# Layer B's in-projections of blocks 1 to 3 as seven half-size products, with weight operands kept in DRAM

## The chip, the cores and the metric

The kernel runs on one core of a Trainium2 chip. The metric is the device time of one execution in microseconds; the time before is the median of three runs. The profile is of one further execution.

## What is computed

One inference step of two layers over 2048 prompt tokens and 64 sample tokens (8 sequences of 8), model width 1024. Layer A (gated DeltaNet) is not changed. Layer B is a retention layer, whose four in-projections take the normed input to queries, keys, values and gates:

```python
p = _rmsnorm(x, norm_w) @ w_in.astype(F32)                 # 1024 -> 2*1024 + 2*2048
q, k, v, gate = jnp.split(p, [B_QK, 2 * B_QK, 2 * B_QK + B_VW], axis=-1)
q = _rotary(q, pos0);  k = _rotary(k, pos0) * (B_DK ** -0.5)   # 4 heads of 256
o, S = _retention_chunked(q, k, v, S0)                     # v: 4 heads of 512, S: 256 x 512
o = _rmsnorm(o, onorm_w) * jax.nn.silu(gate)
y = x + (o.reshape(B, L, B_VW) @ w_out.astype(F32))
```

A final norm follows. The retention states of the prompt and of all sample sequences are outputs too.

## The kernel before

All matrix work is in float32 split into two float32r parts, hi and lo: a product is three matmuls (hi·hi, hi·lo, lo·hi, the table `PASSES`), which accumulate in PSUM. `wload` (L177) loads one raw weight tile of 128 x 1024 into a ring of two buffers named wraw, casts it on ScalarE (hi, L181) and subtracts on VectorE (lo, L182) into a ring of w tiles. `split` (L194, recorded as L195 and L196) does the same for activations.

The prompt is cut into four blocks of 512 tokens (n = 0 to 3). In layer B each block goes through four heads (h = 0 to 3). For a head the program writes, in this order: four gate tiles and two tiles each of Q and K with `colproj` (L236), 24 matmuls of 512 columns each (8 tiles of the inner width by 3 passes); rotation (`rope`, L975); a wait for the last head's retention; V in four PSUM banks, 96 matmuls; then `flush_B` (L1224), the out-projection `outproj_B` (L1153) of the head before, 8 output tiles of 12 matmuls, which adds into the residual xa in SBUF; then the head's own retention `ret_prompt` (L1002) is put on a list of tasks. At h = 3 `build_xn` (L264) makes the next block's normed operands before the out-projection. One head of each block is sampled: its projections are 576 columns wide, as two halves of 288, and `ret_sample` (L1059) follows, which loads and stores 16 state tiles.

The order of the work comes from two places. A list of tasks, `_Pipe` (L36), holds generators with a priority; `pump` runs those whose time has come on a clock that each written matmul moves on, and `wait` runs tasks until one is done. Under it the tile framework schedules the instructions and gives each engine one fixed order. On the chip each engine, and SP's queue of transfers, keeps that order. A buffer of a ring is given out again when everything that read it is done. `pp` (L117) has three PSUM banks, which in-projections and out-projection share; `xst` (L167) is a ring of three 128 x 576 buffers in layer B.

```python
    def wload(src):
        raw = sb.tile([128, 1024], F32, tag="wraw", bufs=2, name="wraw")
        w = wtile()
        nc.sync.dma_start(raw, src)
        ACT.copy(w[:, 0, :], raw)
        V.tensor_tensor(w[:, 1, :], raw, w[:, 0, :].bitcast(F32), op=ALU.subtract)
        return w
```

Of the kernel before, what the change touches and what calls it, by code (L numbers as in the profile page):

```python
# [16 lines left out]
D = 1024  # L17
# [70 lines left out]
def tile_hybrid(ctx: ExitStack, tc: tile.TileContext, a: dict, S: int):  # L88
# [49 lines left out]
    x1_d = dr.tile([D, S + NS], F32, name="x1_d")  # L138

# [25 lines left out]
    wn, xn_ = [0, 2], [0, 3]  # L165
# [700 lines left out]
    wn[1], xn_[1] = 3, 4  # L866
# [83 lines left out]
    def finish_A():  # L950
        wn[:], xn_[:] = [0, 2], [0, 3]
# [9 lines left out]
    def open_B():  # L961
        finish_A()
        pb = ctx.enter_context(tc.tile_pool(name="pb", bufs=1))
        B.pb = pb
        B.rmask = const("rmask", (128, 4, 128), a["rmask"], pb)
# [9 lines left out]
    def rope(pair, c, sn, outs, lo, hi, v=lambda t: t):  # L975
        for (p0, s, e), (p1, _, _) in zip(pieces(pair[0], lo, hi), pieces(pair[1], lo, hi)):
            n = e - s
            for out, (f0, f1), op in ((outs[0], (c, sn), ALU.subtract), (outs[1], (sn, c), ALU.add)):
                t = [sb.tile([128, XC], F32, tag="tmp", bufs=2, name="rt")[:, :n] for _ in range(2)]
                V.tensor_tensor(t[0], p0, f0[:, s:e], op=ALU.mult)  # L980
                V.tensor_tensor(t[1], p1, f1[:, s:e], op=ALU.mult)  # L981
                V.tensor_tensor(out(s, e), v(t[0]), v(t[1]), op=op)
# [19 lines left out]
    def ret_prompt(n, h, QR, KR, Vt, GT, OG):  # L1002
        pb, S_ = B.pb, B.S[h]
        gC = float(gam[h] ** 128)
        for c in range(4):
# [28 lines left out]
            for i, (al, vl) in enumerate(PASSES):  # L1034
                mm(o, Ah[:, al], Vt[:, c, vl], start=(first and i == 0), stop=(i == 2))
            yield from until(posts[-1])
            on = ret_on(o, h, 0)
            for k in range(2):
                p = po("p") if k == 0 else pf("p")
                for i, (al, vl) in enumerate(PASSES):  # L1040
                    mm(p, Kt[:, al, k * 128 : (k + 1) * 128], Vt[:, c, vl], start=(i == 0), stop=(i == 2))
# [17 lines left out]
    def ret_sample(h, QRs, KRs, vraw, GTs, OG, rms):  # L1059
        pb = B.pb  # L1060
        g8 = float(gam[h] ** 8)
# [91 lines left out]
    def outproj_B(h, OG, xa, width, acc):  # L1153
        sacc = B.pb.tile([128, 256], F32, tag="rms", name="sacc")[:, :NS] if h == 0 and width > TB else None
        for cp in range(4):
            w = wload(a["w_out_b"][h, cp])
            for ci in range(2):
# [3 lines left out]
                for p, s, e in pieces(pst, 0, TB):  # L1161
                    V.tensor_tensor(xa[:, ct, s:e], xa[:, ct, s:e], p, op=ALU.add)  # L1162
                if acc is not None:
                    sqsum(acc[:, :TB], xa[:, ct, :], ct)
                if width > TB:
                    (p, _, _), = pieces(pst, TB, XC)
                    V.tensor_tensor(B.xas[:, ct, :], B.xas[:, ct, :], p, op=ALU.add)  # L1167
                    if sacc is not None:
# [308 lines left out]
```

## Time and profile before

| | |
|---|---|
| median of three runs | 3317.8 us (3315.15 to 3319.45) |
| profiled execution | 3320.3 us, span 3318.5 us |
| TensorE busy | 3231.2 us, 97% |
| VectorE, ScalarE, POOL busy | 66%, 44%, 7% |
| DMA | 379.8 MB, 114 GB/s |

The span is the time from the first to the last instruction; the execution's own time is 1.8 us more. Shares of busy time are averages over stages: layer A fills the first part up to some 1430 us, layer B the rest, where a head of a block takes a little over 100 us. The views used below are the page itself, the chain of waits (what work or wait each moment of the end time hangs on), groups of instructions by shape with their mean time, transfers with their time from issue to landing, and tables of busy time by stretch.

### The profile page before, as it was taken

To read this page: it belongs to the slowest core of one execution; us is meant where nothing else is said; L and a number is where in the kernel's file an instruction comes from. 1 tells how busy PE (TensorE), PEld (TensorE's weight loads), DVE (VectorE), ACT (ScalarE), POOL (GpSimd) and SP (SyncE) were. 2 spreads that over 40 slices of the span, in tenths; PEclk is the share of its full clock that TensorE was granted. 3 is DMA by queue.
4 is the path that set the end of the run, shared out by engine and by line. 5 is a ranking of instruction groups with operands and counts; after the bars stand their busy time and mean duration, and the time that the engine had idled before them with its cause. 6 is when DMAs were issued, how large, how long until landed. Compare 5 with 4: busy or idle time off the path is not lost.

```text
span 3318.5 us, 50681 instructions
## 1 busy us (share of the span) xinstructions
PE 3231.2 (97%) x18847; PEld 2700.4 (81%) x18847; DVE 2198.3 (66%) x4943; ACT 1453.5 (44%) x3243; POOL 240.2 (7%) x501
## 2 busy tenths in 40 slices
PE   7999999999999999999999999999999999999998
PEld 7999787778788888788888788877888788878886
DVE  6876778688878877755555665556564656575556
ACT  7655555465545645333333442343342433343333
POOL 1221011001110000000000000000000000000000
PEclk9999999999999999999999999999999999999999
DMA  4333454435444343552223442126232523253222
GB/s 134 96 101 85 144 167 142 132 106 152 130 129 126 89 143 99 151 162 82 74 82 106 129 163 89 59 83 194 77 116 82 171 68 116 71 175 117 89 77 70
DMA packets 241111, 379.78 MB, mean 114 GB/s; under 512 B 100688, under 2 KB 130144, under 8 KB 240864
## 3 DMA queue, kind: packets, MB, share of 16 engines
q1 hardware_dynamic: 240864, 376.54, 37.6%
q8 instruction: 148, 2.42, 0.3%
q14 instruction: 99, 0.81, 0.1%
HBM read 318.90 MB, written 55.46 MB: 113 GB/s over the span
## 4 chain that ended last, share of the span: by engine, by line
PE 83%; DVE 6%; DMA 4%; ACT 3%; POOL 1%; issue 1%; SPq 0%; DVEq 0%; POOLq 0%; ACTq 0%
PE pp L97 53%; PE pv L97 10%; PE o L97 5%; PE p L97 5%; PE kyd L97 2%; PE oT L106 1%; DMA st<-in_state_ret 1%; PE kp L97 1%; DVE w L182 1%; PE ap L97 1%; POOL so L572 1%; PE kq L97 1%; PE os L97 1%; ACT on L569 1%; PE pvs L97 1%
## 5 line engine op out<-in xcount | busy, mean ns | idle before, releaser
L97 PE MATMUL pp<-xn,w 128*128 128x512 f32 (+1 forms) x7760 | 1648.5, 362 | 13.2 <-ACT w L181 4.2
L97 PEld LDWEIGHTS pp<-xn,w 128*128 128x128 f32 x7760 | 1267.3, 189 | 210.2 <-issue 13.9
L181 ACT CAST w<-wraw 128x1024 fp32r<-128x1024 f32 x416 | 436.8, 1050 | 691.4 <-PE pp L97 449.0
L182 DVE TENSOR_TENSOR w<-wraw,w 128x1024 fp32r<-128x1024 f32 x416 | 508.4, 1222 | 249.1 <-ACT w L181 248.0
L97 PE MATMUL pp<-OG,w 128*128 128x512 f32 (+1 forms) x2880 | 582.6, 360 | 6.3 <-DVE xas L1167 3.2
L97 PEld LDWEIGHTS pp<-OG,w 128*128 128x128 f32 x2880 | 482.0, 190 | 89.8 <-issue 3.6
L97 PE MATMUL pv<-w,xn 128*128 128x512 f32 x1536 | 370.8, 396 | 0.0
L97 PEld LDWEIGHTS pv<-w,xn 128*128 128x128 f32 x1536 | 287.1, 188 | 73.8 <-issue 5.0
L1162 DVE TENSOR_TENSOR xa<-xa,pp 128x512 f32<-128x512 f32 (+2 forms) x160 | 90.2, 579 | 137.2 <-PE pp L97 137.1
L728 DVE SCALAR_TENSOR_TENSOR acc<-pp,cw,acc 128x511 f32<-128x511 f32 (+2 forms) x216 | 160.4, 742 | 22.0 <-ACT acc L725 21.7
L990 POOL TENSOR_TENSOR so<-oss,rsc 128x1 f32<-128x1 f32 x72 | 17.8, 247 | 1412.5 <-ACT on L988 1412.5
L981 DVE TENSOR_TENSOR rt<-pp,cs 128x512 f32<-128x512 f32 (+2 forms) x80 | 46.3, 578 | 105.9 <-PE pp L97 105.9
L473 DVE TENSOR_TENSOR VP<-VP,tm 128x66 f32<-128x66 f32 (+26 forms) x510 | 106.5, 209 | 4.4
L471 DVE TENSOR_TENSOR tm<-LP,VP 128x66 f32<-128x66 f32 (+26 forms) x510 | 104.3, 204 | 4.4
L97 PE MATMUL p<-Vt,Kt 128*128 128x512 f32 x384 | 104.4, 405 | 0.6 <-ACT on L992 0.6
L195 ACT CAST OG<-og 128x256 fp32r<-128x256 f32 x192 | 71.7, 405 | 62.0 <-DVE og L628 33.4
L97 PE MATMUL o<-Sc,Qc 128*128 128x512 f32 x360 | 93.4, 394 | 0.0
L196 DVE TENSOR_TENSOR OG<-og,OG 128x256 fp32r<-128x256 f32 x192 | 75.4, 420 | 20.8 <-ACT OG L195 20.5
L106 PE MATMUL oT<-ident,on 128*128 128x128 f32 x432 | 73.1, 276 | 11.4 <-DVE on L573 9.5
L97 PEld LDWEIGHTS p<-Vt,Kt 128*128 128x128 f32 x384 | 68.2, 189 | 13.0 <-ACT on L992 0.9
L106 PEld LDWEIGHTS oT<-ident,on 128*128 128x128 f32 x432 | 52.6, 140 | 31.9 <-DVE on L573 14.6
L97 PEld LDWEIGHTS o<-Sc,Qc 128*128 128x128 f32 x360 | 66.6, 188 | 14.4
(369 smaller groups left out, 3947.3 us busy)
## 6 DMA issues: line engine op xcount, KB each, us to landing
wraw<-in_w_in_a SPq DMA_DIRECT2D x128, 512.0 KB, 3.7
wraw<-in_w_qkg SPq DMA_DIRECT2D x128, 512.0 KB, 3.6
wraw<-in_w_v SPq DMA_DIRECT2D x64, 512.0 KB, 3.7
wraw<-in_w_out_b SPq DMA_DIRECT2D x64, 512.0 KB, 3.6
wraw<-in_w_out_a SPq DMA_DIRECT2D x32, 512.0 KB, 3.7
st<-in_state_ret SPq DMA_DIRECT2D x64, 256.0 KB, 3.6
out_ret_s<-st SPq DMA_DIRECT2D x64, 256.0 KB, 2.7
LP<-sl SPq DMA_DIRECT2D x72, 128.0 KB, 2.9
```

The source lines that it names most:

```text
L97: ins = nc.tensor.matmul(out, lhsT, rhs, start=start, stop=stop)
L106: ins = nc.tensor.transpose(out, x, ident[:p, :p])
L181: ACT.copy(w[:, 0, :], raw)
L182: V.tensor_tensor(w[:, 1, :], raw, w[:, 0, :].bitcast(F32), op=ALU.subtract)
L195: ACT.copy(hi, x)
L196: V.tensor_tensor(lo, x, hi.bitcast(F32), op=ALU.subtract)
L471: V.tensor_tensor(tv, LP[:, m, m + 1 : m + 1 + n].unsqueeze(2).to_broadcast([128, n, ncol]), VP[:, m, 0:ncol].unsqueeze(1).to_broadcast([1 ...
L473: V.tensor_tensor(VP[:, m + 1 : m + 1 + n, 0:ncol], VP[:, m + 1 : m + 1 + n, 0:ncol], tv, op=ALU.subtract)
L569: ACT.activation(on[:, j, :], o[:, j, :], AF.Square, scale=128.0 ** -0.5, accum_out=ss[:, j : j + 1])
L728: V.scalar_tensor_tensor(acc[:, sh:], ap[:, : TB - sh], cw[:, ct, j : j + 1], acc[:, sh:], op0=ALU.mult, op1=ALU.add)
L981: V.tensor_tensor(t[1], p1, f1[:, s:e], op=ALU.mult)
L1162: V.tensor_tensor(xa[:, ct, s:e], xa[:, ct, s:e], p, op=ALU.add)
```

## The change

For blocks 1 to 3 each in-projection of a head is cut in two by two by two: output rows, inner width and tokens in halves. Seven products of half size with sums of weight quarters and of input quarters take the place of eight. The matmuls have 256 columns: 12 in a product of gates, Q or K (`quad`, four per head with seven products each), 24 in one of V (`vquad`, seven products). `seven` adds the products up on VectorE, POOL and ScalarE in temporaries that use the wraw ring: in V the first buffer holds P1, P5 and then U3, the second U2 and U4.

The weight operands (A11, four sums, A12, A22, each as hi and lo) are made once by `prep`, 24 preparations with a task of the lowest priority (9) that starts with `open_B` in block 0. Each loads two weight tiles, forms four sums on POOL, splits seven operands and writes seven slots of 512 KB to DRAM. In blocks 1 to 3 `wstream` loads 42 slots per head into a ring of three w tiles. `build_halves` makes the input operands; three of its tiles have the buffers that `prep` uses (ta, tb, tc), so it waits for the last preparation.

To make room in SBUF, the residual goes through DRAM (x2_d) and the ring xst, the retention state is stored and loaded per head (sr_d), the samples of all four heads are worked in block 0, and V is split per chunk in `ret_prompt`. The task clock counts 0.455 ns a column in the place of 0.4167.

```diff
-        pipe.t += (max(0.4167 * n, 107.0) if rhs.dtype == F32R else max(1.667 * n, 110.0)) / 1000.0
+        pipe.t += (max(0.455 * n, 107.0) if rhs.dtype == F32R else max(1.667 * n, 110.0)) / 1000.0
...
+    x2_d = dr.tile([D, S + NS], F32, name="x2_d")
+    sr_d = dr.tile([BH, 128, 1024], F32, name="sr_d")
+    wh_d = [dr.tile([56, 128, 1024], F32, name=f"wh_d{h}") for h in range(BH)]
...
     def finish_A():
-        wn[:], xn_[:] = [0, 2], [0, 3]
+        wn[:], xn_[:] = [0, 2], [0, 2]
...
     def open_B():
...
+        B.pb = wp[0] = pb
+        wn[1] = 3
...
-        S23 = pb.tile([128, 2, 2, 512], F32, name="S23")
-        B.S = [pb.tile([128, 2, 512], F32, name=f"Sr{h}") for h in range(2)] + [S23[:, 0], S23[:, 1]]
-        B.xas = pb.tile([128, 8, NS], F32, name="xas")
-        nc.sync.dma_start(B.xas, x1_d[:, S : S + NS].rearrange("(k p) t -> p k t", p=128))
...
+    def prep(h, slots, src, vkind):
+        pb = B.pb
+        R = pb.tile([128, 2, 1024], F32, tag="ta", name="Rw")
+        for j in range(2):
+            nc.sync.dma_start(R[:, j, :], src[j])
...
+        yield 4.0
+        PL.tensor_tensor(sm[0], A21, A22, op=ALU.add)
+        PL.tensor_tensor(sm[1], sm[0], A11, op=ALU.subtract)
+        PL.tensor_tensor(sm[2], A11, A21, op=ALU.subtract)
+        PL.tensor_tensor(sm[3], A12, sm[1], op=ALU.subtract)
+        ops = [A11, sm[0], sm[1], A12, sm[2], sm[3], A22]
+        for i, x in enumerate(ops):
+            if i % 2 == 0:
+                o2 = pb.tile([128, 2, 2, 512], F32R, tag="tc", name="Wo")
+            o = o2[:, i % 2]
+            hi, lo = (v3(o[:, j, :], 256) if vkind else o[:, j, :] for j in range(2))
+            split(hi, lo, x)
+            nc.sync.dma_start(wh_d[h][slots[i]], o.rearrange("p t c -> p (t c)").bitcast(F32))
+            yield 1.5
...
+    def wstream(h):
+        for s in range(0, 56, 2):
+            w = wtile()
+            for j in range(2):
+                nc.sync.dma_start(w[:, j, :].bitcast(F32), wh_d[h][s + j])
+            for j in range(2):
+                yield v3(w[:, j, :], 512)
+    def build_halves(n, rb):
...
+        for kt in range(4):
+            xs, t = [], []
+            for k in (kt, kt + 4):
+                x = xst("xs")
+                nc.sync.dma_start(x[:, :TB], x1_d[k * 128 : (k + 1) * 128, n * TB : (n + 1) * TB])
+                y = sb.tile([128, XC], F32, tag="tmp", bufs=2, name="xt")
+                V.scalar_tensor_tensor(y[:, :TB], x[:, :TB], nw[:, 1, k : k + 1], rb[:, :TB],
+                                       op0=ALU.mult, op1=ALU.mult)
+                xs.append(x)
+                t.append(y)
+            lo_, hi_ = xn[kt], xn[kt + 4]
+            split(lo_[:, 0, l], lo_[:, 1, l], t[0][:, l])
+            split(hi_[:, 0, :TB], hi_[:, 1, :TB], t[1][:, :TB])
+            V.tensor_tensor(xs[0][:, l], t[0][:, r], t[0][:, l], op=ALU.subtract)
+            V.tensor_tensor(xs[0][:, r], t[1][:, r], xs[0][:, l], op=ALU.subtract)
+            V.tensor_tensor(xs[1][:, l], t[1][:, r], t[0][:, r], op=ALU.subtract)
+            V.tensor_tensor(xs[1][:, r], t[1][:, l], xs[0][:, r], op=ALU.subtract)
+            split(lo_[:, 0, r], lo_[:, 1, r], xs[0][:, l])
+            split(T2[:, kt, 0], T2[:, kt, 1], xs[0][:, r])
+            split(T3[:, kt, 0], T3[:, kt, 1], xs[1][:, l])
+            split(N4[:, kt, 0], N4[:, kt, 1], xs[1][:, r])
...
+    def seven(product, temp, put):
+        p1, p5, u2, u4 = (temp(j) for j in range(4))
+        ACT.copy(p1, product("b11"))
+        ACT.copy(p5, product("t1"))
+        V.tensor_tensor(u2, product("t2"), p1, op=ALU.add)
+        put(0, 0, product("b21"), p1, V)
+        PL.tensor_tensor(u4, u2, p5, op=ALU.add)
+        u3 = temp(0)
+        V.tensor_tensor(u3, product("t3"), u2, op=ALU.add)
+        put(1, 1, u3, p5, PL)
+        put(0, 1, product("b22"), u4, V)
+        put(1, 0, product("n4"), u3, V)
+    def quad(ws, xo, put):
+        def product(x):
+            w, bank = next(ws), pp("sq")[:, :256]
+            for kt in range(4):
+                for i, (wl, xl) in enumerate(PASSES):
+                    mm(bank, w[:, wl, kt * 128 : (kt + 1) * 128], xo[x](kt, xl),
+                       start=(kt == 0 and i == 0), stop=(kt == 3 and i == 2))
+                if kt % 2:
+                    pipe.pump()
+            return bank
+        temps = sb.tile([128, 1024], F32, tag="wraw", bufs=2, name="ptmp")
+        seven(product, lambda j: temps[:, 256 * j : 256 * j + 256], put)
+    def vquad(ws, xo, Vt):
+        def product(x):
+            w, bank = None, pp("sv")
...
+        temps = [sb.tile([128, 1024], F32, tag="wraw", bufs=2, name="ptmp") for _ in range(2)]
+        seven(product, lambda j: v3(temps[j // 2][:, 512 * (j % 2) : 512 * (j % 2) + 512], 256),
+              lambda i, j, x, y, eng: eng.tensor_tensor(Vt[:, 2 * j : 2 * j + 2, 256 * i : 256 * i + 256], x, y,
+                                                        op=ALU.add))
...
     def ret_prompt(n, h, QR, KR, Vt, GT, OG, S_):
...
+            Vh = pb.tile([128, 2, 512], F32R, tag="Vh", name="Vh")
+            split(Vh[:, 0], Vh[:, 1], Vt[:, c])
...
+        else:
+            nc.sync.dma_start(sr_d[h], S_.rearrange("p k v -> p (k v)"))
...
     def outproj_B(n, h, OG, width, acc):
+        src = x1_d if h == 0 else x2_d
...
+                xs = xst("xr")
+                nc.sync.dma_start(xs[:, :TB], src[rows, n * TB : (n + 1) * TB])
...
+                for p, s, e in pst:
+                    V.tensor_tensor(xs[:, s:e], xs[:, s:e], p[:, : e - s], op=ALU.add)
+                nc.sync.dma_start(x2_d[rows, n * TB : (n + 1) * TB], xs[:, :TB])
...
     def final(n, acc, samp):
...
+            xs = xst("xf")
+            nc.sync.dma_start(xs[:, :TB], x2_d[rows, n * TB : (n + 1) * TB])
...
     for n in range(NB):
         for h in range(4):
-            samp = (3 - h) * NB // 4 == n
+            samp = n == 0
...
+            if n:
+                S_ = pb.tile([128, 2, 512], F32, tag="Sr", bufs=2, name="Sr")
+                nc.sync.dma_start(S_.rearrange("p k v -> p (k v)"), sr_d[h])
+                ws = wstream(h)
...
+                    quad(ws, xo, put)
...
             if start:
                 open_B()
...
+                for j in range(BH):
+                    ptask = pipe.add(prep_head(j), 9, [ptask])
...
             if h == 3 and n + 1 < NB:
-                nxt = build_xn(x1_d, n + 1, 1, rb, XC)
+                pipe.wait(ptask)
+                xo = build_halves(n + 1, rb)
```

Three places of the engines' orders. First SP's queue around a V stage of a late head, before, where a row is a transfer with its target and source:

```order
L180 DMA wraw<-in_w_qkg 128x1024 x3
L1057 DMA out_ret_p<-Sr_16785 128x2x512
L180 DMA wraw<-in_w_qkg 128x1024
L180 DMA wraw<-in_w_v 128x1024 x4
L180 DMA wraw<-in_w_out_b 128x1024 x4
L180 DMA wraw<-in_w_qkg 128x1024 x7
```

and the same with the change, in block 1 (w are the ready operands, wh_d their place in DRAM):

```order
L1206 DMA sr_d<-Sr 128x1024
L1040 DMA w<-wh_d_75 128x1024 x23
L1409 DMA Sr<-sr_d 128x1024
L183 DMA wraw<-in_w_out_b 128x1024 x4
L1319 DMA x_d<-xr 128x512 x2
L1314 DMA xr<-x_d 128x512
```

The out-projection's raw weights stand behind V's weights in both; with the change their first buffer is a temporary of V, and residual tiles are loaded and stored between.

Second, TensorE from the end of a V stage into the out-projection, with the change (sv are V's products, o, p and kT belong to the retention, pp<-OG is the out-projection):

```order
L97 MATMUL sv<-w,tc 128x256 x12
L97 MATMUL ap<-QR,KR 128x128
L97 MATMUL sv<-w,tc 128x256 x12
L97 MATMUL o<-Vh,Ah 128x512
L97 MATMUL p<-Vh,Kt 128x512 x2
L106 MATMUL kT<-ident,KR 128x128
L97 MATMUL o<-Vh,Ah 128x512 x2
L97 MATMUL pp<-OG_23854,w 128x512 x4
L97 MATMUL p<-Vh,Kt 128x512
```

Before, the out-projection follows V's last matmul at once; now five matmuls and a transpose of the head's own retention stand between.

Third, the end of block 0 with the change, on SP (Rw and Wo are a preparation's raw weights and operands, xs the next block's input, xr the residual of the out-projection):

```order
L1003 DMA Rw<-in_w_v 128x1024 x2
L1024 DMA wh_d_76<-Wo 128x1024 x7
L1058 DMA xs<-x_d 128x512 x5
L1314 DMA xr<-x_d 128x512
L1316 DMA xr<-x_d 128x64
```

and on VectorE a little later:

```order
L199 TENSOR_TENSOR ta<-xs,ta 128x256
L199 TENSOR_TENSOR tb<-xs,tb 128x256
L199 TENSOR_TENSOR tc<-xs,tc 128x256
L1318 TENSOR_TENSOR xr<-xr,pp 128x288 x2
L1197 TENSOR_TENSOR og<-oT,GT 128x512 x2
L1318 TENSOR_TENSOR xr<-xr,pp 128x288 x2
```

The six preparations of head 3 stand on SP one behind the other, each two loads and seven writes, this one last; the block's input and the residual of the out-projection come after them, and so do their sums on VectorE.

## Rows read from the trace of the kernel before

**Rows 1.** The page: TensorE, and the span in 40 slices.
```profile
PE 3231.2 (97%) x18847; PEld 2700.4 (81%) x18847; DVE 2198.3 (66%) x4943; ACT 1453.5 (44%) x3243; POOL 240.2 (7%) x501
...
PE   7999999999999999999999999999999999999998
...
PEclk9999999999999999999999999999999999999999
```

**Rows 2.** Chain of waits, a head of block 3: start us, us, what.
```profile
3087.84 20.22 PE pp L97 x87
3108.06 22.32 PE pv L97 x96
3130.39 25.19 PE pp L97 x108
...
3156.24 4.18 PE pp L97 x18
3160.42 2.09 PE o L97 x9
...
3164.57 4.18 PE pp L97 x18
```

**Rows 3.** Busy us by engine, clock, DMA share, GB/s: the same head.
```profile
3088.00:3196.00 108.00, 108.00 (x487) 87.76 (x486) 58.51 (x90) 37.45 (x64) 2.94 (x8) 1.00 0.27 83
```

**Rows 4.** Chain of waits, in-projection of a sampled head, 288 columns.
```profile
1752.11 15.43 PE pp L97 x114
```

**Rows 5.** Groups by shape: xcount | busy us, mean ns | idle before, releaser.
```profile
L181 ACT CAST w<-wraw 128x1024 fp32r<-128x1024 f32 x416 | 436.8, 1050 | 691.4 <-PE pp L97 449.0 <-PE pv L97 121.2 <-PE pvs L97 62.4
...
L195 ACT CAST Sc<-Sr 128x512 fp32r<-128x512 f32 x60 | 35.0, 621 | 7.2 <-PE o L97 6.9
...
L182 DVE TENSOR_TENSOR w<-wraw,w 128x1024 fp32r<-128x1024 f32 x416 | 508.4, 1222 | 249.1 <-ACT w L181 248.0
L196 DVE TENSOR_TENSOR OG<-og,OG 128x256 fp32r<-128x256 f32 x192 | 75.4, 420 | 20.8 <-ACT OG L195 20.5
...
L196 DVE TENSOR_TENSOR Sc<-Sr,Sc 128x512 fp32r<-128x512 f32 x60 | 40.6, 686 | 6.9 <-ACT Sc L195 6.8
...
L1248 POOL MEMSET QRs<- 128x512 f32 x4 | 2.1, 530 | 111.0 <-PE os L97 66.6 <-PE pp L97 44.4
```

**Rows 6.** Transfers: xcount, KB each, median us from issue to landing.
```profile
wraw<-in_w_out_b SPq DMA_DIRECT2D x64, 512.0 KB, 3.6
...
x_d<-xr SPq DMA_DIRECT2D x32, 256.0 KB, 3.3
xs<-x_d SPq DMA_DIRECT2D x32, 256.0 KB, 3.6
...
out_ret_p<-Sr SPq DMA_DIRECT2D x2, 512.0 KB, 2.8
```

**Rows 7.** By stretch: a gap of TensorE and the clock after it.
```profile
2301.40:2304.70 3.30, 0.05 (x2) 0.05 (x1) 3.30 (x7) 1.34 (x2) 0.00 (x0) 1.00 0.43 143
2304.70:2306.00 1.30, 0.76 (x3) 0.53 (x4) 1.30 (x2) 0.00 (x0) 0.00 (x0) 0.88 0.14 50
2306.00:2309.00 3.00, 3.00 (x13) 3.00 (x14) 2.02 (x5) 0.30 (x1) 0.00 (x0) 0.50 0.80 194
2309.00:2312.00 3.00, 3.00 (x23) 2.88 (x23) 0.88 (x3) 0.00 (x0) 0.00 (x0) 0.98 0.39 156
```

**Rows 8.** By stretch: most bytes in 6 us, and in 22 us.
```profile
1482.00:1488.00 6.00, 6.00 (x27) 4.86 (x26) 1.23 (x1) 1.24 (x2) 0.00 (x0) 1.00 1.04 386
...
1479.80:1502.00 22.20, 22.20 (x99) 18.03 (x99) 7.83 (x9) 6.48 (x9) 0.00 (x0) 1.00 0.70 233
```

**Rows 9.** By stretch: a sampled head's in-projection, then the head after it.
```profile
1666.00:1781.00 115.00, 114.31 (x675) 101.95 (x674) 58.87 (x101) 37.29 (x71) 3.77 (x8) 1.00 0.25 75
1781.00:1910.00 129.00, 127.73 (x582) 98.40 (x581) 84.90 (x138) 51.63 (x95) 4.06 (x10) 1.00 0.43 136
```

**Rows 10.** Chain of waits, the end: last matmuls to last output.
```profile
3281.27 21.99 PE pp L97 x93
...
3309.91 0.75 DVE xa L1188
...
3311.32 3.95 DVE xa L1188 x6
```

More of the change, by code (lines that the diff above doesn't have):

```diff
@@ L976, in rope @@
         for (p0, s, e), (p1, _, _) in zip(pieces(pair[0], lo, hi), pieces(pair[1], lo, hi)):
[L977 to L982, printed above, removed]
+            rope_to(p0, p1, c[:, s:e], sn[:, s:e], [out(s, e) for out in outs], v)
@@ new lines, in rope_to, with rope_in @@
+    def rope_to(p0, p1, c, sn, outs, v=lambda t: t):
+        n = c.shape[1]
+        for out, (f0, f1), op in ((outs[0], (c, sn), ALU.subtract), (outs[1], (sn, c), ALU.add)):
+            t = [sb.tile([128, XC], F32, tag="tmp", bufs=2, name="rt")[:, :n] for _ in range(2)]
+            V.tensor_tensor(t[0], p0, f0, op=ALU.mult)
+            V.tensor_tensor(t[1], p1, f1, op=ALU.mult)
+            V.tensor_tensor(out, v(t[0]), v(t[1]), op=op)
+    def rope_in(x, c, sn):
+        t = [sb.tile([128, XC], F32, tag="tmp", bufs=2, name="rt")[:, :TB] for _ in range(2)]
+        V.tensor_tensor(t[0], x[:, 0], c, op=ALU.mult)
+        V.tensor_tensor(t[1], x[:, 1], sn, op=ALU.mult)
+        V.tensor_tensor(x[:, 0], x[:, 0], sn, op=ALU.mult)
+        V.tensor_tensor(x[:, 1], x[:, 1], c, op=ALU.mult)
+        V.tensor_tensor(x[:, 1], x[:, 1], x[:, 0], op=ALU.add)
+        V.tensor_tensor(x[:, 0], t[0], t[1], op=ALU.subtract)
@@ L1034, in ret_prompt @@
             for i, (al, vl) in enumerate(PASSES):
-                mm(o, Ah[:, al], Vt[:, c, vl], start=(first and i == 0), stop=(i == 2))
+                mm(o, Ah[:, al], Vh[:, vl], start=(first and i == 0), stop=(i == 2))
             yield from until(posts[-1])
@@ L1151, in ret_sample, with outproj_B @@
             post(ret_post(on, fin))
-    def outproj_B(h, OG, xa, width, acc):
-        sacc = B.pb.tile([128, 256], F32, tag="rms", name="sacc")[:, :NS] if h == 0 and width > TB else None
+    def outproj_B(n, h, OG, width, acc):
+        src = x1_d if h == 0 else x2_d
         for cp in range(4):
@@ L1182, in final @@
         yield 3.0
[L1183 to L1185 removed]
+        rb = bcast_rstd(rr, rr[:64, 4:5] if samp else None, "rbF")
         for k in range(8):
             rows = slice(k * 128, (k + 1) * 128)
[L1188 to L1189 removed]
@@ L1252, in tile_hybrid @@
-            for d in range(4):
-                if h == 0 and d == 0:
-                    ahead = colproj2([wload(a["w_qkg"][16 + 4 * h + j]) for j in range(2)], xk, width)
-                pst = ahead.pop(0) if ahead else colproj(a["w_qkg"][16 + 4 * h + d], xk, width)
-                for p, s, e in pieces(pst, 0, TB):
-                    ACT.activation(GT[:, d, s:e], p, AF.Silu)
-                V.tensor_scalar(GT[:, d, :], GT[:, d, :], onB[:, h, d : d + 1], None, op0=ALU.mult)
-                if samp:
+            if start:
+                xn_[:] = [0, 2]
+                stash = sb.tile([128, XC], F32, tag="xst2", name="stash")
+                GTs = v3(stash[:, :256], NS)
+                raws = stash[:, 256:512].rearrange("p (k j t) -> p k j t", k=2, j=2)
+            elif samp:
+                GTs = pb.tile([128, 4, NS], F32, tag="GTs", bufs=2, name="GTs")
+                raws = pb.tile([128, 2, 2, NS], F32, tag="raws", name="raws")
@@ L1262, in tile_hybrid @@
                     V.tensor_scalar(GTs[:, d, :], GTs[:, d, :], onB[:, h, d : d + 1], None, op0=ALU.mult)
-                pipe.pump()
+                    pipe.pump()
             for kind in range(2):
                 pair = []
-                for j in range(2):
-                    pair.append(colproj(a["w_qkg"][kind * 8 + 2 * h + j], xk, width, (pp, po)[j]))
-                    pipe.pump()
+                if n == 0:
+                    for j in range(2):
+                        pair.append(colproj(a["w_qkg"][kind * 8 + 2 * h + j], xk, width, (pp, po)[j]))
+                        pipe.pump()
                 if start and kind == 0:
@@ L1276, in tile_hybrid @@
                 dst = ab.tile([128, 2, TB], F32, tag=("X", "gd")[kind], bufs=2, name=("QR", "KR")[kind])
-                rope(pair, cs[:, 0], cs[:, 1], [(lambda s, e, j=j: dst[:, j, s:e]) for j in range(2)], 0, TB)
                 if kind == 0:
```

253 lines of the change are left out of this document (151 added, 102 removed).

## Prediction

> **What bounds the kernel now.** I read the page first, for the engine that is busy. TensorE is busy 97% of the span, and its digits stand at 9 from the second slice on, at the full clock [rows 1]. So in layer B, the second half of the span, time is matmul time, and the chain of waits says of what kind: in one head of block 3 it is one run of in-projection, V projection, out-projection and retention with nothing between [rows 2]. Dividing: 20.22 us for 87 matmuls of 512 columns is 232.4 ns each. The table by stretch shows how much room the others have in such a head of 108 us: VectorE is busy 58.5 us, ScalarE 37.5, DMA a share of 0.27 at 83 GB/s [rows 3]. Work on those three is free here as long as TensorE is not made to wait for it. That decides the reading: what TensorE saves is sure, and what counts is where the change makes it wait.
>
> **1. The products: -68 us.** One head's in-projections are 8 x 24 + 96 = 288 matmuls of 512 columns, 288 x 232.4 ns = 66.9 us. They become 28 products of 12 and 7 of 24 matmuls, 504 of 256 columns. No row has 256-column matmuls of this kind. The nearest is 288: 15.43 us for 114, 135.4 ns [rows 4]. A line through 288 and 512 gives 0.433 ns a column and 121.5 ns at 256, which I take, so 61.2 us. That is 5.7 us a head and 68 us over 12 heads. Bounds: half of 232.4, 116.2 ns, gives -100; no cheaper than 288 columns, 135.4 ns, gives +16. The Trainium skill (TensorE: Matmul & The Clock Gate, Back-to-back issue gap) has columns / 2.4 + 2.5 ns, 109 ns at 256; the rows speak against it, with 232.4 measured at 512 columns where it has 216; by it this term would be about -142.
>
> The weight casts that disappear (12 a head, 1.05 us on ScalarE and 1.22 on VectorE [rows 5]), the sums and copies that come, the split of V that moves into the retention steps, and the state that goes through DRAM cost nothing: VectorE loses 12 x 1.22 = 14.6 us a head and gains about 12 (20 sums of 256 columns, 5 of 512), inside its 49 idle us. Without that cover each sum would cost its 0.4 to 0.7 us. All four heads' sample work moves into block 0; its matmuls are the same in number.
>
> **2. A gap between V and the out-projection: +76 us.** The temporaries of the products take the buffers of the raw weights. The V stage takes both, and the first raw out-projection weight takes the one that holds P5 and U3, which the last sum of V reads. Before, that load was prefetched (the order shows no dependence on V). Now it runs after it: sum 0.7 us and hand-offs 0.3, landing 3.6 [rows 6], cast 1.05, hand-offs 0.2, in all 5.9 us from the last V matmul, of which the order fills 1.3 (five 512-column matmuls, one transpose). That leaves 4.6 us. A gap of 3.3 us in the trace is followed by a clock of 0.5: 1.3 us at 0.88, 3 us at 0.50 and 3 at 0.98 lose 1.7 us of work [rows 7]. So 6.3 us, 12 times, 76. Bounds: 3 us each if half of the landing is hidden, +36; 8.5 if the load queues behind the weight stream, +102.
>
> **3. The preparation that is left over at the end of block 0: +165 us.** This is the largest term. 24 preparations (two loads, four POOL sums, seven hi/lo splits, seven writes of 512 KB) are to run beside block 0. The order shows that 118 of the 168 splits stand ahead of ScalarE's copies of the last V of block 0, and 50 behind, 7.1 preparations. The last 45 follow each other with nothing of another task between. VectorE's first out-projection sums stand behind all of them and behind the new block's operands; SP's loads for those sums too. The out-projection has three PSUM banks, so TensorE stops after 36 of 192 matmuls.
> One preparation: the load of two pieces 3.6 + 1.4 us (512 KB at 386 GB/s [rows 8]), a POOL sum 0.7, cast 0.62, subtraction 0.69 [rows 5], write 2.8 [rows 6], hand-offs 0.3: 10.1 us for the first pair, for there is one operand buffer of two slots and a pair waits for the last pair's two writes. Two more pairs at 0.62 + 2 x 0.69 + 2.8 + 0.3 = 5.1, and the seventh split, 1.5, before the next load: 21.8 us. POOL shows no sum of this shape; the nearest rows are its memset, 0.53, and VectorE's sum, 0.69, which I take; twice that would add 0.7.
> 7.14 x 21.8 = 156 us. Then the operands of block 1: what is left of them is three rounds of a load, 3.6, and some 3.9 us of VectorE (the ring has three buffers, and each round holds two), 24 us with a remainder of 1.3; then the 156 matmuls left, at 135.4 ns, 21, and a first sum, 1: 46. Taken off: the out-projection itself, 192 x 135.4 = 26, and 2.7 retention steps of 4.15 us (8.33 from one step's start to the next less 4.18 of in-projection [rows 2]) that TensorE does meanwhile, 11. 156 + 46 - 26 - 11 = 165. Bounds: transfers that overlap fully, nine of 1.36 us, 12.2 us a preparation, +96; 28 us, with each landing 1.2 us later under load, +213.
>
> **4. The same operands at the next two block ends: +20 us.** Here 24 us of building, then a sum, 1, and five of eight out-projection tiles, 14, stand against 22.3 + 6.3 us of out-projection and gap: about 10 each. Bounds 0 and +40.
>
> **5. Traffic in block 0: +30 us.** From layer B's opening to the last V of block 0 lie about 22 + 3 x 136 us = 430 (115 us for a head with samples, and 129 - 108 more for its retention [rows 9]). 16.9 preparations need 368 us of that in their own chain, and 80 MB of them with 64 MB of weights, states and residuals need 373 us at 386 GB/s [rows 8]. Both fit, the chain and the queue with little to spare, so their delays add. ScalarE, VectorE and SP run in order: a late write holds up the cast of an in-projection weight that stands behind it. Bounds 0 and +110 (landings 1.5 us later everywhere: 28 us x 16.9 = 473, and as much again in mismatched orders).
>
> **6. The weight stream: +12 us.** Each head streams 42 x 0.52 = 22 MB; in V 7.3 MB in 20.4 us, 360 GB/s, against 386 in the best short stretch [rows 8]. Three buffers of 5.8 us of work cover a landing; I take 1 us a head. Bounds 0 and +60. The residual now goes through DRAM in both directions, 16 transfers a head, each 3.3 to 3.6 us [rows 6] in a ring of three: 7.9 us per three tiles of 2.8, hidden just so; it is in the same bounds.
>
> **7. The end: +10 us.** The last eight rows of output are loaded again in rounds of three (load 3.6, scaling 0.7, write 2.8: two more rounds of 7.1) where before 8 x 0.75 us sufficed [rows 10]. Bounds 5 and 15.
>
> **Sum:** -68 + 76 + 165 + 20 + 30 + 12 + 10 = +245. The profiled execution took 3320.3 us, 0.1% over the median of 3317.8; 3320 + 245 = **3565 us**.
>
> **Rivals.**
> - *Overlapped transfers.* The chain of landings is shorter than I add up: the preparation goes at the pace of the transfers, 12.2 us, and the gaps are half as long. -68 + 96 + 36 + 10 + 5 + 5 + 5 = +89: **3409 us**. For it: short stretches do reach 386 GB/s. Against: one operand buffer, which each pair waits for.
> - *Faster.* The preparation costs only VectorE's time, seven subtractions of 0.69 us, 4.8 us each; the writes hold nobody up. Then term 3 is 34 + 46 - 37 = 43. With the other terms at their low ends, -100 + 43 + 36 + 5 = -16: **3304 us**. It decides at 7 us a preparation. Against: each write lands 2.8 us after its issue [rows 6].
> - *DMA becomes the bound.* If streams in layer B go no faster than the 22 us in which the trace moved most, 233 GB/s [rows 8], a head's 22 MB need 94 us against 61.2 + 18.5 of matmuls, +176, and block 0's 144 MB 618 us against 430, +188. With these in the place of terms 5 and 6: **3887 us**. Against: that stretch had a share of 0.70 and was not asked for more.
> - *Products at column time.* Each matmul has a part that falls with its width faster than the line says, -142 in the place of -68: **3491 us**. Against: 288 columns already cost 15 ns more than 288 / 2.4. This is the rule cited under 1.
> - *The change does not save matmul time*, because 256 columns cost what 288 do: +16 in the place of -68, 3649 us, inside my range.
>
> **How the numbers follow.** My forecast has 0.62, with a range of its own of 3470 to 3680; overlapped transfers 0.17; faster 0.10, of which 0.02 within 0.2% (6.6 us, about what a measurement of this kernel can tell from no change); DMA bound 0.07; products at column time 0.04. The range 3400 to 3700 leaves out the faster case, the DMA bound and the edges of the others, 0.2 in all. Faster 0.08, same 0.02, slower 0.90.
>
> **What would show it.** Right: a stretch of over 100 us in the middle of layer B with TensorE near 0 and a lowered clock, ScalarE and VectorE below half busy, waits on writes of prepared operands; twelve idle pieces of 4 to 5 us before out-projection matmuls, released by ScalarE's cast of a weight; 256-column matmuls at some 121 ns. Wrong: TensorE busy through the end of block 0; a preparation under 15 us; the out-projection following V at once; waits for streamed weights inside the products above 3 us a head.

## The result, and the profile after

The changed kernel takes 3691.2 us (median of 4 runs, 3674.8 to 3699.5) against 3317.7 (3315.2 to 3319.5): ratio 1.112, interval 1.108 to 1.116. The profiled execution took 3689.5, its span 3687.7. In the rows PE is TensorE, PEld its weight loads, PEclk its granted clock, DVE is VectorE, ACT ScalarE, POOL GpSimd and SPq the queue of transfers. On the page TensorE falls from 97% to 88%, with a hole at six tenths of the span and a lowered clock around it, where [rows 1] has nines throughout:

```profile
PE 3241.9 (88%) x21436; PEld 2822.0 (77%) x21436; DVE 2348.7 (64%) x5310; ACT 1483.2 (40%) x3463; POOL 480.7 (13%) x714
...
PE   7999999999999999988796603889999999999997
...
PEclk9999999999999999999897856999999999999998
```

The table by stretch, cut at layer B's first V (1515.3), V of block 0's last head (2039.6), the hole, V of block 1's first head (2377.6) and V of the last head (3578.1). Columns as in [rows 3].

```profile
0.00:1515.30 1515.30, 1442.76 (x9914) 1231.82 (x9914) 1135.84 (x3150) 791.35 (x2032) 171.85 (x344) 0.99 0.41 122
1515.30:2039.60 524.30, 426.51 (x2397) 355.41 (x2398) 326.33 (x536) 211.60 (x433) 111.50 (x103) 0.89 0.75 263
2039.60:2103.40 63.80, 52.55 (x227) 40.14 (x225) 45.92 (x81) 28.80 (x57) 14.66 (x14) 0.92 0.57 205
2103.40:2274.20 170.80, 0.08 (x1) 0.08 (x1) 48.54 (x81) 33.12 (x62) 33.19 (x24) 0.50 0.49 185
2274.20:2377.60 103.40, 88.62 (x583) 75.47 (x583) 45.24 (x90) 22.25 (x53) 7.77 (x12) 0.91 0.82 278
2377.60:3578.10 1200.50, 1145.43 (x7855) 1046.67 (x7852) 687.23 (x1279) 363.98 (x767) 135.16 (x206) 0.99 0.82 288
3578.10:3687.70 109.60, 85.93 (x471) 72.36 (x469) 59.63 (x97) 32.05 (x60) 6.55 (x11) 0.91 0.60 205
```

The kernel before has 1475.5, 306.1, 121.7 (up to V of block 1), 1312.3 and 102.9 us for the same five pieces; the first four:

```profile
0.00:1475.50 1475.50, 1420.88 (x9718) 1204.64 (x9719) 1133.58 (x3135) 785.05 (x2017) 173.38 (x344) 0.99 0.43 125
1475.50:1781.60 306.10, 305.41 (x1545) 257.70 (x1544) 160.27 (x258) 105.45 (x191) 10.21 (x25) 1.00 0.29 91
1781.60:1903.30 121.70, 120.85 (x548) 93.92 (x548) 79.37 (x130) 49.36 (x91) 4.06 (x10) 1.00 0.43 132
1903.30:3215.60 1312.30, 1295.13 (x6642) 1072.73 (x6640) 765.89 (x1326) 480.00 (x884) 48.56 (x113) 1.00 0.35 110
```

So 40 us are lost before layer B's first V, 218 in block 0, 216 at its end, 7 at the end of the kernel; 112 are gained in blocks 1 to 3. Part of this only moved, since all sample work now stands in block 0, and the first head's sample projections ahead of the first V (9914 recorded matmuls there, 9718 before); the experiments give the share.

The hole is one wait, and at every other place in blocks 1 to 3 TensorE waits little. Waits of PE, in the hole and from 2404 to 3578 (us in total, times, longest):

```profile
PE pp L97 <- DVE xr L1318: 170.7, 1, 170.7
...
PE sq L97 <- DMA w<-wh_d: 13.3, 18, 2.2
PE o L97 <- ACT Vh L198: 7.2, 6, 1.4
PE pp L97 <- DVE xr L1318: 6.4, 4, 2.3
...
PE pp L97 <- ACT w L184: 3.3, 4, 1.1
```

What stands in the hole: the timeline shows one preparation after another, their loads on SP 24.3 us apart, and within one the pace of a pair, 5.4 us (2126.12 to 2131.57), set by the landing of the last pair's writes:

```profile
2109.04 1.21 SPq L1003 DMA_DIRECT2D Rw<-in_w_qkg  x2
2113.65 0.62 ACT L198 CAST Wo<-Rw 128x512 fp32r<-128x512 f32 x1 [5.77 <-DMA Rw<-in_w_qkg]
...
2114.94 1.26 POOL L1013 TENSOR_TENSOR Sm<-Rw 128x512 f32<-128x512 f32 x1 [14.30 <-DMA Rw<-in_w_qkg]
...
2116.89 1.08 DVE L199 TENSOR_TENSOR Wo<-Sm,Wo 128x512 fp32r<-128x512 f32 x1 [1.90 <-ACT Wo L198]
2117.38 1.71 POOL L1014 TENSOR_TENSOR Sm<-Sm,Rw 128x512 f32<-128x512 f32 x1
2119.17 1.26 POOL L1016 TENSOR_TENSOR Sm<-Rw,Sm 128x512 f32<-128x512 f32 x1
2120.70 0.62 ACT L198 CAST Wo<-Sm 128x512 fp32r<-128x512 f32 x1 [3.84 <-DMA wh_d<-Wo]
...
2126.12 1.14 ACT L198 CAST Wo<-Sm 128x512 fp32r<-128x512 f32 x2 [4.29 <-DMA wh_d<-Wo]
...
2131.57 0.62 ACT L198 CAST Wo<-Rw 128x512 fp32r<-128x512 f32 x1 [4.31 <-DMA wh_d<-Wo]
...
2133.35 1.20 SPq L1003 DMA_DIRECT2D Rw<-in_w_qkg  x2
```

Block 0 has no single hole. There TensorE waits for states, for weight casts and for the retention norm, up to 12.8 us at once, and after such a piece the granted clock is lower (0.89 on average, 1.00 before). The longest piece, and a stretch behind it with TensorE busy throughout at a granted clock of 0.50, the lower of its two levels (1.2 of 2.4 GHz):

```profile
1986.40:1999.20 12.80, 0.09 (x1) 0.00 (x0) 2.17 (x5) 2.52 (x5) 5.41 (x4) 0.58 0.86 309
...
2002.20:2005.20 3.00, 3.00 (x12) 2.85 (x13) 2.74 (x5) 1.38 (x4) 0.00 (x0) 0.50 0.80 302
```

Landings are longer: a raw in-projection weight takes 4.7 us in block 0 against 3.7 in the same stretch of before. The DMA issues of block 0, after:

```profile
wh_d<-Wo SPq DMA_DIRECT2D x111, 512.0 KB, 3.1
Rw<-in_w_qkg SPq DMA_DIRECT2D x24, 512.0 KB, 5.5
wraw<-in_w_qkg SPq DMA_DIRECT2D x24, 512.0 KB, 4.7
st<-in_state_ret SPq DMA_DIRECT2D x48, 256.0 KB, 4.1
```

### The profile page after: what moved, and what is told of

Same layout as the page of the kernel before. It is cut to its first block, busy times and chain, and to the rows that moved or that the text cites. A ratio compares the mean times of both kernels' runs of the same rounds, so it can differ in the third digit from the quotient of the medians.

```text
span 3687.7 us, 58945 instructions
## 1 busy us (share of the span) xinstructions
PE 3241.9 (88%) x21436; PEld 2822.0 (77%) x21436; DVE 2348.7 (64%) x5310; ACT 1483.2 (40%) x3463; POOL 480.7 (13%) x714
## 5 line engine op out<-in xcount | busy, mean ns | idle before, releaser
L97 PE MATMUL pp<-xn,w 128*128 128x288 f32 (+1 forms) x5456 | 1113.0, 353 | 41.0 <-ACT w L184 10.6
L97 PEld LDWEIGHTS pp<-xn,w 128*128 128x128 f32 x5456 | 865.9, 194 | 151.2 <-issue 14.0
L97 PE MATMUL pp<-OG,w 128*128 128x512 f32 (+1 forms) x2880 | 597.4, 365 | 194.5 <-DVE xr L1318 177.4
L97 PEld LDWEIGHTS pp<-OG,w 128*128 128x128 f32 x2880 | 491.0, 194 | 283.0 <-DVE xr L1318 181.2
L185 DVE TENSOR_TENSOR w<-wraw,w 128x1024 fp32r<-128x1024 f32 x272 | 337.6, 1243 | 105.0 <-ACT w L184 101.3
L184 ACT CAST w<-wraw 128x1024 fp32r<-128x1024 f32 x272 | 285.7, 1051 | 175.0 <-PE pp L97 104.0
L97 PE MATMUL sq<-xn,w 128*128 128x256 f32 x2304 | 311.9, 286 | 15.9 <-DMA w<-wh_d 13.3
L97 PEld LDWEIGHTS sq<-xn,w 128*128 128x128 f32 x2304 | 292.0, 191 | 25.9 <-DMA w<-wh_d 8.6
L97 PE MATMUL sv<-w,xn 128*128 128x256 f32 x1152 | 149.1, 284 | 1.2 <-DMA w<-wh_d 1.0
L97 PEld LDWEIGHTS sv<-w,xn 128*128 128x128 f32 x1152 | 143.1, 188 | 5.2 <-DVE rt L989 1.7
L97 PE MATMUL o<-Sc,Qc 128*128 128x512 f32 x360 | 114.3, 409 | 17.0 <-ACT Sc L198 13.6
L97 PE MATMUL p<-Vh,Kt 128*128 128x512 f32 x384 | 113.6, 408 | 0.8 <-ACT Kt L1157 0.4
L97 PE MATMUL pv<-w,xn 128*128 128x512 f32 x384 | 96.7, 402 | 6.6 <-DVE rt L982 3.6
```

## The experiments

All runs are compared with the kernel before on the same chip, at 3318 to 3319 us. "The stretch" is from layer B's first V to V of block 1, block 0 and its end together: 862 us after the change. The same matmuls stand in it in every kernel below (3192 to 3205 of them are recorded), so its length can be compared.

**1. One preparation of 24.**

```diff
-                for j in range(BH):
-                    ptask = pipe.add(prep_head(j), 9, [ptask])
+                ptask = pipe.add(prep(0, range(7), [a["w_qkg"][16 + i] for i in range(2)], False), 9)
-                nc.sync.dma_start(w[:, j, :].bitcast(F32), wh_d[h][s + j])
+                nc.sync.dma_start(w[:, j, :].bitcast(F32), wh_d[0][(s + j) % 7])
```

> Leaves out 23 of the 24 preparations: only the first seven operands are made, and every head streams those seven from DRAM in place of its own, so the products are computed with the wrong weights while their number, sizes and bytes stay. Theory (the preparation is what costs): the gap of 170 us at the end of block 0 goes and that head falls from 338 to some 136 us, -202; block 0, from its first V to its last, falls from 524 us to some 375 to 410, -115 to -150. With 3691 that makes 3340 to 3375 us. Rival (block 0 is slow because the sample work and its state loads now all stand there, whatever is prepared): only the gap goes, 3480 to 3500 us.

Measured 3378.4 us (3370.2 to 3382.5), 3 us over the range of the theory. Block 0 takes 398 us, its end 147, with no idle piece of TensorE over 4 us:

```profile
1510.30:1908.60 398.30, 386.01 (x2397) 332.79 (x2397) 230.11 (x433) 155.18 (x329) 22.54 (x43) 1.00 0.53 173
1908.60:2055.50 146.90, 129.11 (x801) 109.81 (x799) 92.48 (x196) 50.95 (x116) 9.61 (x18) 0.97 0.68 228
```

The theory holds: the preparation costs 313 us; in the profiled executions block 0 loses 126 by it and its end 191. Of the 126, some 86 are idle time of TensorE and 40 are the same 2397 recorded matmuls at a lower clock, 426.5 us at 0.89 after the change and 386.0 at 1.00 here. That all heads now stream the same seven operands is not what makes it faster: blocks 1 to 3 take 1203.5 us, 1200.5 after the change. And without the preparation the change is still 60 us slower than the kernel before.

**2. The planning constant.** `0.455` back to `0.4167` in `mm`.

> Undoes one part: the constant by which the order of the work is planned, 0.455 us per 1000 columns back to 0.4167. Theory: V of the first head of layer B starts 40 us later than before because the other constant orders layer A's tasks differently; with the old one it starts within 10 us of 1475.5 plus what open_B adds, and the time is 3650 to 3675 us. Rival (the 40 us come from the start of layer B, two transfer buffers in place of three and the work put ahead of V): 3685 to 3700 us, V's start within 5 us of 1515.

Measured 3660.7 us (3653.3 to 3664.5); layer B's first V stands at 1481.6:

```profile
0.00:1481.60 1481.60, 1424.50 (x9914) 1217.40 (x9914) 1135.56 (x3150) 786.95 (x2030) 173.22 (x344) 1.00 0.42 124
```

Against the same row of after, 18 us of TensorE's busy time and 15 us of its idle time are gone, with the same 9914 matmuls: the constant reorders layer A, and that costs 34 of the 40 us. The other 6 go with the sample projections that now stand there. In layer B it works the other way: the hole grows to 232.5 us, since 66 splits are now behind V in place of 50, and block 0 shortens by 50.

**3. GpSimd's queue.** The two `nc.sync.dma_start` of `prep` become `PL.dma_start`.

> The loads and writes of the preparation are issued by GpSimd in place of SP; nothing else. Theory: block 0 is slow because SP takes its transfers in order, and state and weight loads stand behind writes that wait for a split; then block 0 falls by 60 to 100 us, the gap at its end stays at 150 to 180 us, and the time is 3590 to 3630 us. Rival 1 (the bytes, or ScalarE and VectorE in order, slow it): 3675 to 3705 us. Rival 2 (GpSimd now waits for the splits, and the power for the retention norm stands behind it): block 0 longer than 524 us, 3700 to 3800 us.

Measured 3778.5 us (3769.9 to 3792.6), in rival 2's range, but not by its way alone: block 0 is 513 us, a little shorter, and the hole 284.7. GpSimd waits 240 us in block 0 for splits, fewer preparations get done there (93 writes in place of 111), and one takes 30 us in the hole:

```profile
2201.20 1.05 POOL L1003 DMA_DIRECT2D Rw<-in_w_qkg  x2
...
2208.00 0.54 POOL L1024 DMA_DIRECT2D wh_d<-Wo  x1 [5.74 <-DVE Wo L199]
...
2218.54 1.13 POOL L1024 DMA_DIRECT2D wh_d<-Wo  x2 [4.09 <-DVE Wo L199]
2224.57 1.13 POOL L1024 DMA_DIRECT2D wh_d<-Wo  x2 [4.90 <-DVE Wo L199]
...
2231.24 1.06 POOL L1003 DMA_DIRECT2D Rw<-in_w_qkg  x2
```

SP free of the preparation does not make block 0 fast: TensorE's wait for states is 22.7 us, 26.4 before the edit.

**4. No writes.** `prep` writes only the first seven operands, and all heads stream them as in 1.

> Leaves out the writes of the prepared operands (all but the first seven); every head streams those seven, so the products have the wrong weights. Loads, sums and splits stay. Theory: without the writes a preparation has no wait for a buffer and takes some 15 us in place of 24.3; the gap shrinks from 170.7 to 105 to 120 us; SP waits no more for splits and 84 MB leave block 0, which falls by 60 to 115 us: 3520 to 3580 us. Rival (ScalarE and VectorE in order are what slows block 0): only the gap shrinks, and block 0 by 20 us at most, 3615 to 3640 us.

Measured 3508.8 us (3506.4 to 3512.7), 182 less and 11 under the range of the theory. Block 0 takes 455 us, the hole is 52 us, smaller than expected, because only 29 splits stand behind V; a preparation takes 14.6 us there. TensorE's wait for states in block 0 is 4.3 us. In the order of the change, the writes are 182 of the 313 us; loads, sums and splits are the other 131.

**5. Four operand slots.** The operands alternate between two buffers; block 0 has two weight buffers again.

```diff
-                o2 = pb.tile([128, 2, 2, 512], F32R, tag="tc", name="Wo")
+                o2 = pb.tile([128, 2, 2, 512], F32R, tag=("tc", "w2")[on_[0] % 2], name="Wo")
```

> The operands of the preparation get a second buffer (four slots in place of two): in block 0 the weights go back to two buffers and the third's place is the operands'. The order has 38 splits behind V of block 0's last head in place of 50, 5.4 preparations. Theory (the wait of a pair for the last pair's landings sets the pace): a preparation takes 16 to 18 us in place of 24.3, the gap falls from 170.7 to 85 to 110 us, block 0 (first V to last) from 524 to 490 to 520, and the time is 3580 to 3625 us. Rival (bytes set the pace; the landings get longer as they overlap): the gap stays over 140 us, 3655 to 3690 us.

Measured 3631.4 us (3621.2 to 3634.5). A preparation at the end takes 18.8 us (loads at 2109.51 and 2128.30), the holes there are 33 and 54 us. But block 0 grew to 544 us: its raw weights land after 5.1 us (4.7 in after) and TensorE waits 29 us for their casts. The time is between the two ranges: the preparation is faster, its end gains 73 us, and block 0 loses 20 of them. The weight buffer that block 0 gave up does not show as the reason, since ScalarE's casts wait 24 us there for a free one, against 26 after the change; the longer landings are what its rows leave, and no run tests them by themselves.

**6. Later writes.** The `dma_start` of `prep` behind its `yield 1.5` in place of ahead of it.

> Each write of a prepared operand is issued one step later, so that the split is done when SP comes to it; nothing else. The order has 62 splits behind V of block 0's last head in place of 50, so the gap grows by some 43 us. Theory (SP, in order, holds up state and weight loads behind writes that wait): TensorE's wait for states in block 0 falls from 26 us to under 10, block 0 from 524 us to 440 to 480; 3650 to 3695 us. Rival (landings are longer because of the bytes, and ScalarE and VectorE are held up by the splits): block 0 stays at 495 to 525 us; 3705 to 3735 us.

Measured 3686.8 us (3672.3 to 3692.7), no change. Block 0 is 485 us, between the two, but the hole is 207.9: what block 0 gained its end lost, 867 us for the stretch against 862. TensorE's wait for states is still 21 us. A later place for the writes in SP's order does not shorten the stretch.

**7. One preparation, and the old constant in layer A.** Experiment 1 with `0.455` set in `open_B`, `0.4167` ahead of it.

> Two edits: as in the run with one preparation, 23 of 24 are left out (wrong weights in the products, their number, sizes and bytes as they were), and the constant 0.4167 stands in layer A, 0.455 in layer B alone. It prices the change with the preparation for nothing. Theory (the two costs are apart): 3378 less 30 to 35, 3343 to 3350 us, still 0.7 to 1.0% slower than before, since idle pieces take more than the products save. Rival (layer A's gain is given back at the start of layer B): 3365 to 3380 us. Other rival (the constant was the rest of it): 3310 to 3325 us.

Measured 3344.2 us (3341.0 to 3350.2), ratio 1.0075 (1.0052 to 1.0098): 34 us below experiment 1, so the two costs are apart. This is what the change is worth with the preparation nearly free.

**8. The preparation rearranged.** One task for all 24:

```diff
-            ops = [A11, sm[0], sm[1], A12, sm[2], sm[3], A22]
+            ops = [(0, A11), (3, A12), (6, A22), (1, sm[0]), (2, sm[1]), (4, sm[2]), (5, sm[3])]
...
+                if i % 2:
+                    yield 1.5
+                    write()
+                    if i == 3 and g + 1 < len(jobs):
+                        nxt = load(jobs[g + 1])
```

> The preparation rearranged, output as in the reference: four operand slots, the three pieces that need no sum split first, the next pieces loaded as soon as these are read, writes issued a step later, two splits a step; 0.4167 as the planning constant in layer A. The order has none of the 168 splits behind V of block 0's last head. Theory (chain and order, not bytes, make the 313 us of the preparation): the gap is gone, that head takes 147 to 165 us, block 0 430 to 470; 3345 plus 35 to 90, 3380 to 3435 us. Rival (bytes): 138 MB now stand in block 0 and its end, at the 263 GB/s of block 0 524 us, so block 0 takes 510 to 560 us; 3460 to 3520 us.

Measured 3570.7 us (3564.6 to 3578.9). As its order said, the hole is gone: the last head takes 152 us. But block 0 takes 625, more than the rival said, and the time is over both ranges. TensorE waits there for raw weights' casts (65 us) and for states (47); ScalarE waits 165 us for landed writes, and the casts stand behind it in order. Block 0 has one weight buffer fewer here too, but the casts wait only 11 us for a free one. The stretch is 777 us at 272 GB/s.

**9. Half the bytes.** In 8, `wh_d[h][slot][:, :512]` is written from the high half alone, and streamed twice.

> As the rearranged preparation, but each write carries the high half alone, 256 KB in place of 512, and the stream reads that half twice (the low halves of the products' weights are left out, so their values are wrong; splits, waits, number of transfers and the stream's bytes stay). In the rearranged kernel the stretch from layer B's first V to that of block 1 took 777 us, with one preparation 547. Theory (bytes): 42 of about 210 MB go, at 270 GB/s 155 us; the stretch takes 620 to 660 us, the time is 3415 to 3455 us. Rival (a write holds its buffer for the same time whatever it carries, and ScalarE and VectorE stand behind it in order): the stretch stays over 735 us, 3530 to 3570 us.

The stretch is 659 us, within 1 us of the theory's range: 118 us less for 44 MB. The run does not say by which way bytes cost: with half the bytes a write also lands sooner, after 3.7 us in place of 4.5, and ScalarE waits less for it. First the rearranged kernel, then this one:

```profile
ACT Wo L199 <- DMA wh_d<-Wo: 164.7, 48, 10.9
```
```profile
ACT Wo L199 <- DMA wh_d<-Wo: 62.0, 29, 8.3
```

The time, 3490.6 (3487.1 to 3494.4), lies between the two forecasts, because blocks 1 to 3 now take 1244 us: the stream of halves read twice has 64,512 packets more on the page and lands after 5.8 us in place of 5.2, and from block 1's second head on TensorE waits 26 us for it in place of 11.

**10. Sums only.** The four sums are written unsplit, the other three operands come from the weights, and every streamed tile is split at use; the products' temporaries get buffers of their own:

```diff
+            raw = sb.tile([128, 1024], F32, tag="wraw", bufs=2, name="wraw")
...
+            split(w[:, 0, :], w[:, 1, :], raw)
```

> Output as in the reference. The preparation writes only the four sums of each quad, unsplit, in one transfer of 1 MB; the three other operands are streamed from the weights as they lie, and ScalarE and VectorE split each streamed tile as the kernel before did (21 pairs a head). 48 MB in place of 108 are prepared, a head streams 11 MB in place of 22; 0.4167 as the constant in layer A. Theory (the bytes and splits in block 0 are what the preparation costs): first V to V of block 1 falls from 862 us to 570 to 610; blocks 1 to 3 stay within 30 us of 1200, since VectorE goes from 57% to some 80%: 3370 to 3430 us. Rival (the splits at use become the wait of the products: load 3.6, cast 1.05, subtraction 1.24 and 2.85 of use per tile against a ring of three): blocks 1 to 3 take 1250 to 1350 us, 3440 to 3560 us.

Measured 3483.0 us (3480.0 to 3485.8), the best version that leaves nothing out. The theory and its rival both hold, each for its stretch: 606 us for the stretch, and 1285 for blocks 1 to 3, where VectorE is busy 74% (57% after) and TensorE's largest wait is for its sums:

```profile
2086.30:3371.20 1284.90, 1180.40 (x7861) 1068.09 (x7860) 945.78 (x1514) 587.67 (x1003) 163.73 (x206) 0.97 0.55 176
```
```profile
PE sq L98 <- DVE ptmp L1099: 30.7, 8, 5.6
```

The stretch in all these kernels, from its row by stretch and its DMA table:

| kernel | us | MB | GB/s | TensorE busy |
|---|---|---|---|---|
| after | 862 | 211 | 245 | 568 |
| later writes | 867 | 211 | 244 | 560 |
| four slots | 809 | 212 | 262 | 583 |
| rearranged | 777 | 211 | 272 | 582 |
| half the bytes | 659 | 167 | 254 | 560 |
| no writes | 681 | 127 | 186 | 546 |
| sums only | 606 | 140 | 230 | 539 |
| one preparation | 547 | 102 | 187 | 517 |

With the bytes unchanged, order and buffers bring 862 down to 777; with order unchanged in turn, fewer bytes bring 777 to 659. "No writes" with the old order and 127 MB takes longer than "half the bytes" with 167. So it is both: the order and the buffers, in the change itself a chain of landings with two slots, and the bytes with the landings that depend on them. At 272 GB/s the stretch is near the 288 at which blocks 1 to 3 run all the time.

## Why the prediction was right, and where it was not

The direction, the mechanism of the largest term and the range held, the range by 9 us; the narrower 3470 to 3680 that the forecast gave itself was missed by 11. That it was not missed by more is partly luck, for the sum has errors of both signs. Of the 373 us lost, 245 were forecast. The runs split them in three: preparation 313 (forecast, terms 3 and 5: 195), the constant in layer A 34 (nothing), all the rest 25 (terms 1, 2, 4, 6, 7: 50).

- **Term 3, the hole, +165: right, 10 to 16% short.** One idle piece of 170.7 us, TensorE at 0, released by the first out-projection sum. The term counts from V's last matmul to the out-projection's end, 202 us less 37 of work done meanwhile; the row has 230 less 48, 182 us of idle time:

```profile
2067.50:2297.60 230.10, 48.13 (x262) 41.81 (x262) 78.15 (x133) 53.88 (x105) 41.91 (x34) 0.60 0.51 184
```

  By experiment 1 the preparation costs 191 there. A preparation takes 24.3 us, not 21.8. In the timeline above the second piece of its load is there after 5.9 us, not 5.0, the first sum on GpSimd takes 1.26 us, not 0.7, VectorE's subtraction beside one 1.08, not 0.69, and each later pair 5.4, not 5.1; the sum of 1.71 us is not on the chain, since the split behind it waits for a landing. The Trainium skill (GPSIMD Engine Reference, Elementwise — side-by-side cycle accounting) has such an addition, at 2048 columns, 1.96 times as long on GpSimd as on VectorE; an estimate by it is 0.69 x 1.96 = 1.35 us, and the row's 1.26 is near it.
- **Term 5, traffic in block 0, +30: the step that failed.** Measured +126, over its bound of 110. "Both fit, the chain and the queue with little to spare, so their delays add" took fitting for being nearly free. In a stretch where 75% of the DMA time is taken each landing is a microsecond longer, the engines that split and cast take things in order, and TensorE idles in many pieces of 1 to 13 us, 86 of the 126 us; behind those the clock is lower, which the term did not have: that is the other 40 (experiment 1).
- **Not in the sum: layer A, +34.** The diff's first line changes the constant by which all the program is ordered, and I priced only what follows the opening of layer B. What layer A computes is not changed, but its order is. It needed no run to see that the edit stands there; only its price did.
- **Term 2, the gap between V and the out-projection, +76: wrong.** The chain of waits in a head of block 3 shows V's end, and the out-projection 3 us later, with retention matmuls in all but 1.4 of them:

```profile
3391.40 1.43 PE sv L97 x12
3392.86 0.70 DVE Vt L1124
3393.58 0.63 ACT Vh L198
3394.25 0.50 PE o L97
...
3395.80 0.93 PE pp L97 x4
3396.73 0.23 PE p L97
3396.97 21.43 PE pp L97 x92
```

  The first raw weight was issued at 3390.36, when the last sum but one had been read:

```profile
3389.64 0.69 DVE L1124 TENSOR_TENSOR Vt<-sv,ptmp 128x512 f32<-128x512 f32 x1 [2.25 <-PE sv L97]
3390.36 0.33 SPq L183 DMA_DIRECT2D wraw<-in_w_out_b  x1
```

  So it took the buffer of U2 and U4, which that sum reads, not that of P5 and U3, as the prediction has it; only the second load (3393.69) waits for the last sum. Waits of this kind sum to 13 us in blocks 1 to 3 (Vh 7.2, ScalarE's cast 3.3, VectorE's 2.6), and 1.4 us of idling was not followed by a lower clock here (1.00 over this head).
- **Term 1, the products, -68: right in kind, a little short.** A run of them is `3451.48 4.99 PE sq L97 x42`, 118.8 ns; 504 a head are 59.9 us against 66.9, -84 over 12 heads. The trace does not bear out the 109 ns of the rule cited (the Trainium skill, TensorE: Matmul & The Clock Gate, Back-to-back issue gap), which that section gives for an isolated matmul, without the time of its weight load. The 118.8 lies between half of the 512-column time, 116.2, and the line's 121.5. By it both rivals on the products' price fall. What reaches the time is less: a plain head of block 3 goes from 107.7 to 102.9 us.
- **Terms 4, 6 and 7, +20, +12 and +10: right, 4 somewhat high.** Waits for out-projection sums and the last row sum add up to under 10 us, those for streamed weights to 13.6, with 4.0 for residuals in front of products, and the end is 6.7 us longer.
- **The rivals.** Overlapped transfers fall with 24.3 us a preparation. "Faster" falls twice: at its price of the preparation, and since even one preparation of 24 leaves 3344 us. DMA as the bound was half right: not in blocks 1 to 3, which run at 288 GB/s with 13.6 us of waiting, but as a part of what slows block 0.

The errors of the sum partly cancelled: preparation and layer A cost 152 us more than forecast, terms 1 and 2 some 80 less. The change without preparation and constant is left with 25 us, where its terms as measured add up to about -35: some 60 us stand in no term, and runs do not take them apart. By the rows of experiment 7, against those of before, TensorE's busy time up to the last V falls by 55 us in layer B, and its idle time grows by 66, from 19 to 85:

```profile
1482.60:2030.00 547.40, 516.80 (x3196) 442.74 (x3196) 323.50 (x628) 206.08 (x444) 32.05 (x61) 0.98 0.57 187
2030.00:3233.90 1203.90, 1149.58 (x7858) 1050.57 (x7859) 684.78 (x1277) 364.24 (x767) 135.30 (x206) 0.99 0.82 288
```

## What to carry to other kernels

Work moved to a place "beside" other work is free only while nothing there waits on it in order: price the engines that take things in order, the landings under the load that the move itself makes, and the clock behind the idle pieces, not only the sums of busy time and bytes. A form that saves matmul time but multiplies operands must pay for making, writing and reading them: here 84 us of matmuls stood against 313. And a constant of the planner is an edit of the whole program: look at the order everywhere it reaches.

## What was not expected of the hardware

In the timelines above a GpSimd sum of 128 x 512 takes 1.26 to 1.71 us, and VectorE's subtraction of the same shape, 0.69 alone, takes 1.08 beside it, and 2.30 in four places of experiment 3. The Trainium skill (SBUF — State Buffer, Terms) says the two engines have a port pair that one of them holds for a whole instruction; 0.39 us more beside a sum of 1.26 agrees with a part of such a wait; no run here separates it from another cause. Issued by GpSimd, the pair of writes that sets the preparation's pace comes every 6.0 us in place of 5.4. The same bytes streamed in pieces of half the size, each read twice (experiment 9), land 0.6 us later.
